# Two attention layers on one Trainium2 core: the first layer's projection steps as one stream, matrix work in program order, and edits to the order around them

## The chip, the cores and the metric

The kernel runs on one core of one Trainium2 chip. The metric is the device time of one execution in microseconds (us), lower is better. The engines of the core work beside each other, each on its own list of instructions in a fixed order: TensorE (PE in the rows, with its weight loads as PEld), VectorE (DVE), ScalarE (ACT), GpSimd (POOL) and SyncE (SP), which here does nothing but issue DMAs.

## What is computed

A decoder of two layers on 512 tokens of width 1024, in float32. The first layer ("fox") is causal attention with a learned decay, the second is latent attention (MLA) with rotary parts; each is followed by a gated feed-forward block.

```python
def fox_attention(xn, w_in, b_f, w_o):
    proj = xn @ w_in                      # q, k, v of 16 heads of 64, and a forget gate
    ...
    log_f = jax.nn.log_sigmoid(f_logit.astype(jnp.float32))
    cum = jnp.cumsum(log_f, axis=1)
    o = causal_block_attention(q, k, v, 1.0 / math.sqrt(FOX_HEAD_DIM), cum)
    return o.reshape(B, S, FOX_WIDTH) @ w_o
```

`causal_block_attention` is q·k times a scale, plus the difference of the two cumulated decays, masked, through a softmax over the keys, times v. The MLA layer does the same without the decay; its q and k have 96 columns a head, of which 32 are rotated.

## The kernel before

**Number format.** Each float32 matrix is held as a sum of two reduced-precision parts, hi and lo. A product is three matmuls (`mm3`, lines 375 to 378: hi·hi, hi·lo, lo·hi). The hi part of a weight is a cast on ACT (line 201), its lo part a subtraction (line 202) on DVE or, for the second half of a shared weight, on POOL. Weights come by one DMA of 512 KB each (line 238, SP's queue).

**A fox head.** Heads come in eight pairs (pair 0 to 7; heads 2p and 2p+1 are pair p). For the head *n*, `attention` (line 497) issues the scores of head *n*+1 first, then transposes of the softmax blocks of head *n* (`T_FIRST`, seven 128x128 blocks), then one dense step, then the last three blocks (`T_LAST`), the rest of the dense steps, and the products with V (`values`, eight matmuls into tile `o`). The softmax of a head is, for each of four blocks of rows, a maximum (DVE, line 439), an exponential (ACT, line 445), a reciprocal (DVE, line 452) and a multiplication (POOL line 454, DVE line 457 for the wider parts). A transposed block goes into its hi part (ACT, line 473) and its lo part (DVE, line 474). `o` is drained by ACT (line 486) and DVE (`oraw`, line 487). `T_LAST` and `o` share one PSUM buffer, so that `T_LAST` of a head can start only when `oraw` of the head before has been read out.

**The dense steps beside the heads ("fills").** While the heads run, PE also computes what later heads need. A pair's q and its k are a unit each, of four steps of six matmuls 512 wide (`qk_units`, line 714; tile `qkp`). Behind the fourth step of a unit `qk_parts` (line 694) makes its float32 form (DVE, `qf`, line 696), its hi part (ACT, line 698), its lo part (DVE, line 699) into a tile `hl` that has two buffers, and copies these by DMA from SP (lines 706 and 707 for q, 709 and 710 for k) into the operand tile `qk` of each of the two heads; two small rows of decay follow (lines 691 and 692). There are three `qk` tiles, used in turn. The scores of head 2p therefore need: the last matmul of pair p's k, then DVE, ACT, DVE, SP and the landing of the DMA. A V unit (eight steps of 12 matmuls 256 wide, from `v_unit`) serves four heads and is made in pairs 3 and 5. In the tail the output projection (`out_step`, line 548) fills the place of the q and k steps, as `wo` matmuls.

**What sets the order.** `distribute` (line 489) puts the steps of pair p into the heads 2p-3 and 2p-2, in equal shares. The order on each engine is then made by the scheduler of the framework: within PE, too, it can move an instruction ahead of one that stands earlier in the program. In before, this is what happens: the scores of the next pair, which the program writes right behind `values`, stand on PE some 6 us of work behind the last step of that pair's k. In the MLA layer a part of each head (lines 522 to 534) has a written order on ACT and DVE.

Of the kernel before, what the change touches and what calls it, by code (L numbers as in the profile page):

```python
# [9 lines left out]
F32 = mybir.dt.float32  # L10
F32R = mybir.dt.float32r
# [3 lines left out]
ALU = mybir.AluOpType  # L15
AX = mybir.AxisListType

P = 128
S = 512
# [143 lines left out]
def yoco_fox_mla_kernel(  # L163
# [325 lines left out]
    def distribute(fills, steps, at):  # L489

        share = sum(c for c, _ in steps) / len(at)
        done = 0.0
        for c, f in steps:
            fills.setdefault(at[min(int((done + 0.5 * c) / share), len(at) - 1)], []).append(f)
            done += c

    def attention(att, order, passes, v, oT, fills, split_softmax):

        n_heads = 2 * len(order)
        att.scores(passes(0))
        att.softmax((0, 1))
        att.softmax((3, 2))
        for f in fills.get(-1, []):
            f()
        for n in range(n_heads):
            p, hb = divmod(n, 2)
            more = n + 1 < n_heads
            if more:  # L510
                att.scores(passes(n + 1))
            att.transposes(T_FIRST)
            beside = fills.get(n, [])
            if more and split_softmax:
                att.softmax((0, 1))
            for f in beside[:1]:
                f()

            if split_softmax or not more:
                att.transposes(T_LAST)  # L520
                if more:
                    att.softmax((3, 2))
            else:
                att.softmax((0,))
                att.maximum(3)
                with tc.manual_schedule(engines={mybir.EngineType.Activation, mybir.EngineType.DVE}):
                    att.transposes(T_LAST)
                    att.maximum(1)
                    att.exponential(1)
                    att.exponential(3)  # L530
                    att.maximum(2)
                    att.exponential(2)
                for qb in (1, 3, 2):
                    att.normalise(qb)
            for f in beside[1:]:
                f()
            if hb == 0:
                oraw = tmp_tile("oraw")
            att.values(v(n), oraw, hb)
            if hb == 1:  # L540
                pp = order[p]
                ACT.copy(out=oT[:, 0, pp, :], in_=oraw)
                (POOL if more else DVE).tensor_tensor(
                    out=oT[:, 1, pp, :], in0=oraw, in1=oT.bitcast(F32)[:, 0, pp, :], op=ALU.subtract)
        for f in fills.get(n_heads, []):
            f()

# [126 lines left out]
    with ExitStack() as fx:  # L674
# [39 lines left out]
        def qk_units(pp, seq):  # L714
            steps = []
            for w, key in enumerate(("q", "k")):
                st = {}
                for c in range(4):
                    def go(c=c, w=w, key=key, st=st):
                        if c == 0:  # L720
                            st["w"] = getw((key, pp))
                            st["o"] = bank(ps_mm, "qkp")
                        dense(st["o"], st["w"], xs, [2 * c, 2 * c + 1], c == 0, c == 3)
                        if c == 3:
                            qk_parts(pp, seq, w, st["o"])
                    steps.append((6 * 0.216, go))
            return steps

        def run(steps):
            for _, f in steps:  # L730
                f()
# [65 lines left out]
            decay_rows(qk[hb].bitcast(F32), 2 * FOX_PAIRS[0] + hb)  # L797
        run(v1[7:])
        ahead = qk_units(FOX_PAIRS[1], 1)
        run(ahead[:2])  # L800

        oT = new_xs("oT_fox")
        wo_open = {}
        fills = {}
        for p in range(1, NPAIR):
            steps = ahead[2:] if p == 1 else qk_units(FOX_PAIRS[p], p)
            if p in (3, 5):
                qd = (p + 1) // 2
                steps += v_unit(lambda hf, q_=FOX_QUADS[qd]: ("v", q_, hf), xs, KT, 2, vts[qd], vtiles, norm)
            distribute(fills, steps, [-1, 0] if p == 1 else [2 * p - 3, 2 * p - 2])  # L810
        for at, m, c0, c1 in ((13, 0, 0, 6), (14, 1, 0, 6), (15, 0, 6, 7), (15, 1, 6, 7), (15, 2, 0, 2), (16, 2, 2, 5)):
            fills.setdefault(at, []).append(out_step("fwo", wo_open, oT, FOX_PAIRS, m, c0, c1))

        def fox_passes(n):
# [111 lines left out]
    with ExitStack() as fx:  # L926
# [54 lines left out]
        def rope_keys(krf):  # L981
            r = slice(0, ROPE)
            sw = tmp_tile("sw")
            DVE.stream_shuffle(sw[r], krf[r], SWAP)
            POOL.tensor_tensor(out=sw[r], in0=sw[r], in1=rope_s[r], op=ALU.mult)
            DVE.tensor_tensor(out=krf[r], in0=krf[r], in1=rope_c[r], op=ALU.mult)
            DVE.tensor_tensor(out=krf[r], in0=krf[r], in1=sw[r], op=ALU.add)
            krs = mp.tile([P, 2, S], F32R, name="krs", tag="rr", bufs=1)
            ACT.copy(out=krs[r, 0, :], in_=krf[r])
            DVE.tensor_tensor(out=krs[r, 1, :], in0=krf[r], in1=krs.bitcast(F32)[r, 0, :], op=ALU.subtract)  # L990
            for q in range(2):
                SP.dma_start(out=kr.bitcast(F32)[q * 64:(q + 1) * 64, :],
                             in_=krs.bitcast(F32)[r, q:q + 1, :].broadcast_to([ROPE, 2, S]))
# [87 lines left out]
        def rope_unit(qd):  # L1081
            def done(o):
                raw = tmp_tile("qr")
                if qd == 0:
                    DVE.tensor_tensor(out=raw, in0=o, in1=state["qrow"], op=ALU.mult)
                else:
                    ACT.copy(out=raw, in_=o)
                sw = tmp_tile("sw")
                DVE.stream_shuffle(sw, raw, SWAP)
                POOL.tensor_tensor(out=sw, in0=sw, in1=rope_s, op=ALU.mult)  # L1090
                DVE.tensor_tensor(out=raw, in0=raw, in1=rope_c, op=ALU.mult)
                DVE.tensor_tensor(out=raw, in0=raw, in1=sw, op=ALU.add)
                rr = mp.tile([P, 2, S], F32R, name="rr", tag="rr", bufs=1)
                ACT.copy(out=rr[:, 0, :], in_=raw)
                DVE.tensor_tensor(out=rr[:, 1, :], in0=raw, in1=rr.bitcast(F32)[:, 0, :], op=ALU.subtract)
                state["rr"] = rr
            return uq_unit(qd, 2, done)
# [22 lines left out]
        for p in range(1, NPAIR):  # L1120
# [17 lines left out]
                fills[11] = steps_f(uv[2:])  # L1138
                continue
            distribute(fills, steps, [-1, 0] if p == 1 else [2 * p - 3, 2 * p - 2])  # L1140
        for at, m, c0, c1 in ((12, 0, 0, 4), (13, 0, 4, 6), (13, 1, 0, 2), (14, 1, 2, 6), (15, 0, 6, 7), (15, 1, 6, 7),
                              (15, 2, 0, 2), (16, 2, 2, 5)):
            fills.setdefault(at, []).append(out_step("mwo", wo_open, oT, range(NPAIR), m, c0, c1))

# [130 lines left out]
```

## Time and profile before

| | |
|---|---|
| time, median of three runs | 1227.26 us (1226.89 to 1228.17) |
| the profiled execution | 1227.15 us |
| its span (first to last instruction in the profile) | 1225.4 us |
| PE busy in the span | 1211.3 us (99%) |
| DVE, ACT, POOL busy | 721.5 us (59%), 532.3 us (43%), 232.7 us (19%) |
| stretch of the fox heads | about 46 to 236 us |
| stretch of the MLA heads | about 670 to 824 us |

The profiled execution's time is 1.75 us longer than its span, and 0.11 us under the median of the runs. Busy times of PE are modelled a little long: a row can end after the next row of the same engine starts, so that distances between starts tell more than busy shares. In a timeline row the number in front is the start, then comes the length, the engine, the line and what is written and read; a bracket at the end is the engine's idle time before the row, and what released it.

### The profile page before, as it was taken

What the parts mean: (1) busy time and instruction counts of PE and PEld (TensorE: products, weight loads), DVE (VectorE), ACT (ScalarE), POOL (GpSimd) and SP (SyncE); (2) the same over time, 40 slices, a digit from 0 to 9 for tenths busy, and PEclk for the clock granted to TensorE, in tenths of its full rate; (3) what the DMA queues carried; (4) which work ended last, traced back from release to release, by engine and by line L of the source; (5) the groups of instructions that cost most, each with busy time, mean ns of one, the idle gap of its engine ahead of it and who ended that gap; (6) DMA issues with size and microseconds to landing.
All of it is one profiled execution on the core that took longest, in us unless ns stands there. A gap on an engine that the chain in (4) does not pass through costs nothing.

```text
span 1225.4 us, 16578 instructions
## 1 busy us (share of the span) xinstructions
PE 1211.3 (99%) x5959; PEld 1018.0 (83%) x5959; DVE 721.5 (59%) x1497; ACT 532.3 (43%) x1149; POOL 232.7 (19%) x268
## 2 busy tenths in 40 slices
PE   9999999999999999999999999999999999999997
PEld 7889888788888888888898888888888888888886
DVE  7776777645454554633467899967454545552323
ACT  6565556533233232322363577755333333332322
POOL 2333323211111111000012233322011111110100
PEclk9999999999999999999999999999999999999999
DMA  7554644223333323333324767714323232323322
GB/s 243 131 148 122 154 112 116 86 86 103 93 97 103 101 89 97 103 95 95 106 76 118 184 173 180 183 60 125 99 88 100 89 103 87 103 87 102 95 78 69
DMA packets 49890, 137.23 MB, mean 112 GB/s; under 512 B 5840, under 2 KB 10960, under 8 KB 49808
## 3 DMA queue, kind: packets, MB, share of 16 engines
q1 hardware_dynamic: 47264, 134.31, 38.1%
q10 hardware_dynamic: 2544, 1.87, 0.5%
q8 instruction: 47, 0.77, 0.3%
q14 instruction: 35, 0.29, 0.1%
HBM read 104.30 MB, written 2.10 MB: 87 GB/s over the span
## 4 chain that ended last, share of the span: by engine, by line
PE 93%; DVE 2%; DMA 2%; ACT 1%; issue 1%; POOL 1%; SPq 0%; ACTq 0%; POOLq 0%; DVEq 0%
PE dn L378 19%; PE dn L376 19%; PE dn L377 18%; PE s L427 4%; PE dn L1208 3%; PE dn L1207 3%; PE dn L1209 3%; PE o L483 3%; PE t L469 3%; PE qkp L376 2%; PE qkp L378 2%; PE qkp L377 2%; PE vv L586 1%; PE vv L585 1%; PE vv L584 1%
## 5 line engine op out<-in xcount | busy, mean ns | idle before, releaser
L201 ACT CAST whi<-wstage 128x512 fp32r<-128x512 f32 (+2 forms) x382 | 212.2, 601 | 450.5 <-issue 237.2
L202 DVE TENSOR_TENSOR wlo<-wstage,whi 128x512 fp32r<-128x512 f32 (+2 forms) x364 | 280.1, 805 | 111.4 <-ACT whi L201 111.2
L376 PE MATMUL dn<-xs,whi 128*128 128x512 f32 x704 | 275.1, 391 | 0.0
L378 PE MATMUL dn<-xs,wlo 128*128 128x512 f32 x704 | 274.0, 389 | 0.0
L377 PE MATMUL dn<-xs,whi 128*128 128x512 f32 x704 | 273.9, 389 | 0.0
L378 PEld LDWEIGHTS dn<-xs,wlo 128*128 128x128 f32 x704 | 132.1, 188 | 27.7
L376 PEld LDWEIGHTS dn<-xs,whi 128*128 128x128 f32 x704 | 132.2, 188 | 27.1
L377 PEld LDWEIGHTS dn<-xs,whi 128*128 128x128 f32 x704 | 132.2, 188 | 27.0
L857 POOL TENSOR_TENSOR u<-u,g 128x512 f32<-128x512 f32 x44 | 68.8, 1564 | 424.9 <-DVE u L856 379.6
L856 DVE TENSOR_TENSOR u<-dn,inv_row 128x512 f32<-128x512 f32 x44 | 30.4, 691 | 146.9 <-PE dn L378 146.9
L454 POOL TENSOR_SCALAR p<-p,rs 128x128 f32<-128x128 f32 (+1 forms) x128 | 63.6, 503 | 153.0 <-DVE rs L452 134.5
L445 ACT ACTIVATE p<-s,nm 128x512 f32<-128x512 f32 (+3 forms) x128 | 67.0, 529 | 38.5 <-DVE nm L439 31.3
L853 DVE TENSOR_TENSOR g<-dn,inv_row 128x512 f32<-128x512 f32 x44 | 30.4, 691 | 68.7 <-PE dn L378 68.7
L439 DVE CUSTOM_DVE_ANT_0 s<-s,mask 128x128 f32<-128x128 f32 (+3 forms) x128 | 61.0, 499 | 9.8 <-PE s L427 9.8
L340 POOL TENSOR_TENSOR acc<-acc,sq 128x512 f32<-128x512 f32 x22 | 33.2, 1507 | 161.4 <-ACT sq L339 161.2
L474 DVE TENSOR_TENSOR pt<-t,pt 128x384 fp32r<-128x384 f32 (+1 forms) x96 | 54.2, 593 | 7.4 <-ACT pt L473 6.8
L473 ACT CAST pt<-t 128x384 fp32r<-128x384 f32 (+1 forms) x96 | 46.6, 519 | 17.5 <-PE t L469 17.1
L376 PE MATMUL qkp<-xs_fox,whi 128*128 128x512 f32 x128 | 52.3, 409 | 0.0
L378 PE MATMUL qkp<-xs_fox,wlo 128*128 128x512 f32 x128 | 50.3, 393 | 0.0
L377 PE MATMUL qkp<-xs_fox,whi 128*128 128x512 f32 x128 | 49.8, 389 | 0.0
L469 PE MATMUL t<-ident,p 128*128 128x128 f32 x320 | 47.0, 274 | 2.4 <-POOL p L454 1.4
L469 PEld LDWEIGHTS t<-ident,p 128*128 128x128 f32 x320 | 38.2, 140 | 12.5 <-POOL p L454 3.7
(283 smaller groups left out, 2327.7 us busy)
## 6 DMA issues: line engine op xcount, KB each, us to landing
wstage<-in_weights SPq DMA_DIRECT2D x160, 512.0 KB
qk<-hl SPq DMA_DIRECT2D x32, 256.0 KB
mqk<-hl SPq DMA_DIRECT2D x16, 512.0 KB
wstage<-in_weights SPq DMA_DIRECT2D x16, 448.0 KB
wstage<-in_weights SPq DMA_DIRECT2D x10, 576.0 KB
qk<-hl SPq DMA_DIRECT2D x32, 128.0 KB
mqk<-rr SPq DMA_DIRECT2D x32, 128.0 KB
mqk<-hl SPq DMA_DIRECT2D x16, 256.0 KB
```

The source lines that it names most:

```text
L201: ACT.copy(out=hi[:, a:b], in_=stage[:, a:b])
L202: (POOL if shared and a else DVE).tensor_tensor(out=lo[:, a:b], in0=stage[:, a:b], in1=hi.bitcast(F32)[:, a:b], op=ALU.subtract)
L376: PE.matmul(o, lhsT=wh, rhs=xh, start=start, stop=False)
L377: PE.matmul(o, lhsT=wh, rhs=xl, start=False, stop=False)
L378: PE.matmul(o, lhsT=wl, rhs=xh, start=False, stop=stop)
L427: PE.matmul(t[:, off:off + n], lhsT=a[:, qb * P:(qb + 1) * P], rhs=b[:, 0:n], start=(i == 0), stop=(i == len(passes) - 1))
L439: DVE.tensor_tensor_reduce(out=sv, in0=sv, in1=mask[:, S - n:S], scale=1.0, scalar=BIG, op0=ALU.add, op1=ALU.min, accum_out=self.small[1][ ...
L445: ACT.activation(out=pv, in_=sv, func=AF.Exp, bias=nm[:, qb:qb + 1], scale=-1.0, accum_out=ssum[:, qb:qb + 1])
L454: POOL.tensor_scalar(out=pv[:, :cut], in0=pv[:, :cut], scalar1=r, scalar2=1.0, op0=ALU.mult, op1=ALU.mult)
L469: PE.transpose(t[:, i * P:(i + 1) * P], self.p[:, POFF[qb] + kb * P:POFF[qb] + (kb + 1) * P], ident)
L474: DVE.tensor_tensor(out=self.pt[1][:, sl], in0=t[:, :n], in1=self.pt[0].bitcast(F32)[:, sl], op=ALU.subtract)
L857: POOL.tensor_tensor(out=u, in0=u, in1=g, op=ALU.mult)
```

## The change

- The fox layer's steps of q, k and V are one list. Three steps (two before) of pair 1 run ahead of the heads; the others are dealt to the heads -1 to 12 by a fixed table of counts, 4 4 4 4 5 6 7 6 5 7 6 6 3 2, so that most pairs are made earlier than before.
- All of `attention` is under a manual schedule for PE: PE runs in the order in which the program is written. The other engines stay with the scheduler, but for two parts of the MLA heads.
- In the fox layer, where a head has four steps or more, two of them (one before) stand ahead of `T_LAST`.
- The output projection's steps are cut anew in both layers and begin in head 12 of fox.
- In the MLA layer, the split of a pair's output (`split_out`) comes a head later, and on POOL behind the first normalisation of the softmax; the head before the last takes the fox form of the softmax.
- Two rotary buffers become double, and a parameter for a scratch size goes from 1024 to 512.

```diff
+    def attention(*args):
+        with tc.manual_schedule(engines={mybir.EngineType.PE}):
+            attention_heads(*args)
...
+        def split_out(oraw, pp, eng):
+            ACT.copy(out=oT[:, 0, pp, :], in_=oraw)
+            eng.tensor_tensor(out=oT[:, 1, pp, :], in0=oraw, in1=oT.bitcast(F32)[:, 0, pp, :], op=ALU.subtract)
...
-            if more and split_softmax:
+            in_parts = split_softmax or n == n_heads - 2
+            if more and in_parts:
                 att.softmax((0, 1))
-            for f in beside[:1]:
+            ahead = 2 if split_softmax and len(beside) >= 4 else 1
+            for f in beside[:ahead]:
                 f()
...
-                att.softmax((0,))
+                att.maximum(0)
+                att.exponential(0)
+
+                with tc.manual_schedule(engines={mybir.EngineType.Pool}):
+                    att.normalise(0)
+                    if late is not None:
+                        split_out(*late)
+                        late = None
...
-            if hb == 1:
-                pp = order[p]
-                ACT.copy(out=oT[:, 0, pp, :], in_=oraw)
-                (POOL if more else DVE).tensor_tensor(
-                    out=oT[:, 1, pp, :], in0=oraw, in1=oT.bitcast(F32)[:, 0, pp, :], op=ALU.subtract)
+            if hb == 1 and more and not split_softmax:
+                late = oraw, order[p], POOL
+            elif hb == 1:
+                split_out(oraw, order[p], POOL if more else DVE)
...
-        run(ahead[:2])
+        run(ahead[:3])
...
-        for p in range(1, NPAIR):
-            steps = ahead[2:] if p == 1 else qk_units(FOX_PAIRS[p], p)
+
+        steps = ahead[3:]
+        for p in range(2, NPAIR):
+            steps += qk_units(FOX_PAIRS[p], p)
             if p in (3, 5):
...
-            distribute(fills, steps, [-1, 0] if p == 1 else [2 * p - 3, 2 * p - 2])
-        for at, m, c0, c1 in ((13, 0, 0, 6), (14, 1, 0, 6), (15, 0, 6, 7), (15, 1, 6, 7), (15, 2, 0, 2), (16, 2, 2, 5)):
+        for at, n in enumerate((4, 4, 4, 4, 5, 6, 7, 6, 5, 7, 6, 6, 3, 2)):
+            fills[at - 1] = [f for _, f in steps[:n]]
+            steps = steps[n:]
+        assert not steps
+        for at, m, c0, c1 in ((12, 0, 0, 3), (13, 0, 3, 6), (13, 1, 0, 3), (14, 1, 3, 5), (14, 1, 5, 6), (14, 0, 6, 7), (15, 1, 6, 7), (15, 2, 0, 2), (16, 2, 2, 5)):
...
-            krs = mp.tile([P, 2, S], F32R, name="krs", tag="rr", bufs=1)
+            krs = mp.tile([P, 2, S], F32R, name="krs", tag="rr", bufs=2)
...
-                rr = mp.tile([P, 2, S], F32R, name="rr", tag="rr", bufs=1)
+                rr = mp.tile([P, 2, S], F32R, name="rr", tag="rr", bufs=2)
```

In the rows of the instruction orders below, a name's number tells tiles of one name apart; numbers of before and of the change don't correspond. A row with x4 stands for four alike.

PE, where pair 7's k (`qkp`) ends and head 14's scores (`s` from `qk2`) come, before:

```order
L378 MATMUL qkp_2282<-xs_fox_130,wlo_2170 128x512
L483 MATMUL o_2337<-pt0_274,v_1771 128x512
...
L469 MATMUL t_2360<-ident_83,p_276 128x128 x4
L469 MATMUL t_2367<-ident_83,p_276 128x128 x3
L376 MATMUL wo_2392<-oT_fox_637,whi_2276 128x512
...
L469 MATMUL t_2411<-ident_83,p_276 128x128 x3
L427 MATMUL s_2349<-qk2_264 128x256 x4
```

PE at the same place in the change:

```order
L469 MATMUL t_2303<-ident_83,p_276 128x128 x3
L376 MATMUL qkp_2235<-xs_fox_130,whi_2123 128x512
...
L378 MATMUL qkp_2235<-xs_fox_130,wlo_2124 128x512
L376 MATMUL wo_2346<-oT_fox_643,whi_2229 128x512
...
L483 MATMUL o_2357<-pt0_274,v_1773 128x512
...
L427 MATMUL s_2369<-qk2_264 128x256 x4
```

Before, eight matmuls of `o`, seven transposes, 18 matmuls of `wo` and three more transposes stand between the two; in the change nine matmuls of `wo` and the eight of `o`.

PE, where pair 2's k ends and head 4's scores (`s` from `qk1`) come, before (`qkp_951` is k of pair 2, `qkp_1061` q of pair 3):

```order
L378 MATMUL qkp_951<-xs_fox_130,wlo_839 128x512
L483 MATMUL o_1006<-pt0_274,v_279 128x512
...
L469 MATMUL t_1036<-ident_83,p_276 128x128 x3
L376 MATMUL qkp_1061<-xs_fox_130,whi_945 128x512
...
L469 MATMUL t_1068<-ident_83,p_276 128x128 x3
L376 MATMUL qkp_1061<-xs_fox_130,whi_945 128x512
...
L427 MATMUL s_1018<-qk1_263 128x256 x4
```

PE at the same place in the change (`qkp_888` is k of pair 2, `qkp_999` q of pair 3):

```order
L469 MATMUL t_955<-ident_83,p_276 128x128 x3
L376 MATMUL qkp_888<-xs_fox_130,whi_776 128x512
...
L378 MATMUL qkp_888<-xs_fox_130,wlo_777 128x512
L376 MATMUL qkp_999<-xs_fox_130,whi_882 128x512
...
L469 MATMUL t_1006<-ident_83,p_276 128x128 x3
L376 MATMUL qkp_999<-xs_fox_130,whi_882 128x512
...
L483 MATMUL o_1035<-pt0_274,v_279 128x512
...
L427 MATMUL s_1047<-qk1_263 128x256 x4
```

`T_LAST` (three transposes) now stands behind twelve matmuls of steps where six stood, and `o` ahead of the scores comes behind it.

DVE, where pair 6's k is drained, before:

```order
L457 TENSOR_SCALAR p_276<-p_276,rs_2048 128x384
L452 RECIPROCAL rs_2048<-ssum_2046 128x1
L457 TENSOR_SCALAR p_276<-p_276,rs_2048 128x256
L696 TENSOR_TENSOR qf_2106<-qkp_2065,inv_row_397 128x512
L202 TENSOR_TENSOR wlo_2387<-wstage_2167,whi_2386 128x512 x2
L699 TENSOR_TENSOR hl_2108<-qf_2106,hl_2108 128x512
```

DVE at the same place in the change (line 717 is the former 696, line 720 the former 699):

```order
L474 TENSOR_TENSOR pt1_275<-t_2086,pt0_274 128x384
L717 TENSOR_TENSOR qf_2108<-qkp_2018,inv_row_397 128x512
L452 RECIPROCAL rs_2065<-ssum_2063 128x1
L202 TENSOR_TENSOR wlo_2341<-wstage_2121,whi_2340 128x512
L457 TENSOR_SCALAR p_276<-p_276,rs_2065 128x384
L202 TENSOR_TENSOR wlo_2341<-wstage_2121,whi_2340 128x512
L720 TENSOR_TENSOR hl_2110<-qf_2108,hl_2110 128x512
```

A reciprocal and a multiplication of the softmax now stand between `qf` and the lo part of `hl`; before, they stood ahead of `qf`.

## Rows read from the trace of the kernel before

**Rows 1.** The chain that ended last, share of the span by engine.

```profile
PE 93%; DVE 2%; DMA 2%; ACT 1%; issue 1%; POOL 1%; SPq 0%; ACTq 0%; POOLq 0%; DVEq 0%
```

**Rows 2.** Stretches: length, then busy PE, PEld, DVE, ACT, POOL, clock, DMA share, GB/s.

```profile
46.00:236.00 190.00, 187.76 (x1065) 161.47 (x1064) 140.36 (x365) 113.92 (x279) 64.90 (x89) 1.00 0.45 115
670.00:824.00 154.00, 151.91 (x878) 130.83 (x877) 136.14 (x385) 102.87 (x273) 46.12 (x75) 1.00 0.62 156
```

**Rows 3.** Waits of PE from 46 to 236 us: total us, times, longest.

```profile
PE t L469 <- DVE oraw L487: 0.8, 3, 0.3
PE t L469 <- POOL p L454: 0.6, 1, 0.6
PE s L427 <- issue: 0.5, 2, 0.2
```

**Rows 4.** Timeline, pair 2's last k matmul (80.16) to the scores of head 4.

```profile
80.16 0.39 PE L378 MATMUL qkp<-xs_fox,wlo 128*128 128x512 f32 x1
80.39 1.44 PE L483 MATMUL o<-pt,v 128*128 128x512 f32 x8
80.58 0.69 DVE L696 TENSOR_TENSOR qf<-qkp,inv_row 128x512 f32<-128x512 f32 x1 [1.08 <-PE qkp L378]
81.58 1.44 POOL L202 TENSOR_TENSOR wlo<-wstage,whi 128x512 fp32r<-128x512 f32 x1 [1.84 <-ACT whi L201]
81.66 0.93 PE L469 MATMUL t<-ident,p 128*128 128x128 f32 x7
82.05 1.51 DVE L699 TENSOR_TENSOR hl<-qf,hl 128x512 fp32r<-128x512 f32 x1 [0.18 <-ACT hl L698]
...
83.58 0.40 PE L378 MATMUL qkp<-xs_fox,wlo 128*128 128x512 f32 x1
83.59 1.32 SPq L709 DMA_DIRECT2D qk<-hl  x2
84.22 0.55 PE L469 MATMUL t<-ident,p 128*128 128x128 f32 x3 [0.24 <-DVE oraw L487]
...
85.74 1.13 SPq L238 DMA_DIRECT2D wstage<-in_weights  x1
...
86.44 0.39 PE L378 MATMUL qkp<-xs_fox,wlo 128*128 128x512 f32 x1
87.08 1.31 PE L427 MATMUL s<-qk 128*128 128x256 f32 x7 [0.24 <-issue]
```

**Rows 5.** Timeline, pair 6: its last k matmul drained, to the scores of head 12.

```profile
178.84 0.69 DVE L696 TENSOR_TENSOR qf<-qkp,inv_row 128x512 f32<-128x512 f32 x1 [1.10 <-PE qkp L378]
179.45 1.28 DVE L202 TENSOR_TENSOR wlo<-wstage,whi 128x512 fp32r<-128x512 f32 x2
...
180.66 0.68 DVE L699 TENSOR_TENSOR hl<-qf,hl 128x512 fp32r<-128x512 f32 x1
...
185.17 1.06 PE L427 MATMUL s<-qk 128*128 128x256 f32 x6
```

**Rows 6.** Timeline of an MLA head near the layer's end (POOL, DVE, PE).

```profile
798.62 1.28 POOL L543 TENSOR_TENSOR oT_mla<-oraw,oT_mla 128x512 fp32r<-128x512 f32 x1 [2.15 <-ACT oT_mla L542]
...
798.92 0.16 DVE L452 RECIPROCAL rs<-ssum 128x1 f32<-128x1 f32 x1
...
799.88 0.37 POOL L454 TENSOR_SCALAR p<-p,rs 128x128 f32<-128x128 f32 x1
...
800.30 0.33 PE L469 MATMUL t<-ident,p 128*128 128x128 f32 x1 [0.85 <-POOL p L454]
...
802.11 0.43 DVE L457 TENSOR_SCALAR p<-p,rs 128x384 f32<-128x384 f32 x1
```

**Rows 7.** A stretch after PE's last matmul (columns as in Rows 2).

```profile
1221.00:1222.00 1.00, 0.00 (x0) 0.00 (x0) 0.36 (x1) 0.39 (x1) 0.00 (x0) 0.62 0.00 0
```

**Rows 8.** Timeline of PE, the first matmuls of the program.

```profile
1.25 5.36 PE L298 MATMUL pg<-warm 128*128 128x512 bf16 x13 [1.25 <-DVE warm L285]
```

More of the change, by code (lines that the diff above doesn't have):

```diff
@@ L495, in distribute, with attention_heads @@
             done += c
-    def attention(att, order, passes, v, oT, fills, split_softmax):
+    def attention(*args):
+        with tc.manual_schedule(engines={mybir.EngineType.PE}):
+            attention_heads(*args)
+    def attention_heads(att, order, passes, v, oT, fills, split_softmax):
         n_heads = 2 * len(order)
+        late = None
+        def split_out(oraw, pp, eng):
+            ACT.copy(out=oT[:, 0, pp, :], in_=oraw)
+            eng.tensor_tensor(out=oT[:, 1, pp, :], in0=oraw, in1=oT.bitcast(F32)[:, 0, pp, :], op=ALU.subtract)
         att.scores(passes(0))
@@ L513, in attention @@
             beside = fills.get(n, [])
-            if more and split_softmax:
+            in_parts = split_softmax or n == n_heads - 2
+            if more and in_parts:
                 att.softmax((0, 1))
-            for f in beside[:1]:
+            ahead = 2 if split_softmax and len(beside) >= 4 else 1
+            for f in beside[:ahead]:
                 f()
-            if split_softmax or not more:
+            if in_parts or not more:
                 att.transposes(T_LAST)
@@ L522, in attention @@
                     att.softmax((3, 2))
-            else:
-                att.softmax((0,))
+                if late is not None:
+                    split_out(*late)
+                    late = None
+            else:
+                att.maximum(0)
+                att.exponential(0)
+                with tc.manual_schedule(engines={mybir.EngineType.Pool}):
+                    att.normalise(0)
+                    if late is not None:
+                        split_out(*late)
+                        late = None
                 att.maximum(3)
-                with tc.manual_schedule(engines={mybir.EngineType.Activation, mybir.EngineType.DVE}):
+                with tc.manual_schedule(engines={mybir.EngineType.Activation, mybir.EngineType.DVE, mybir.EngineType.PE}):
                     att.transposes(T_LAST)
@@ L534, in attention @@
                     att.normalise(qb)
-            for f in beside[1:]:
+            for f in beside[ahead:]:
                 f()
@@ L1140, in yoco_fox_mla_kernel @@
             distribute(fills, steps, [-1, 0] if p == 1 else [2 * p - 3, 2 * p - 2])
-        for at, m, c0, c1 in ((12, 0, 0, 4), (13, 0, 4, 6), (13, 1, 0, 2), (14, 1, 2, 6), (15, 0, 6, 7), (15, 1, 6, 7),
+        for at, m, c0, c1 in ((12, 0, 0, 2), (12, 0, 2, 4), (13, 0, 4, 6), (13, 1, 0, 2), (14, 1, 2, 4), (14, 1, 4, 6), (15, 0, 6, 7), (15, 1, 6, 7),
                               (15, 2, 0, 2), (16, 2, 2, 5)):
@@ L1257 @@
     from concourse.bass_utils import run_bass_kernel_spmd
-    nc = bacc.Bacc("TRN2", target_bir_lowering=False, num_devices=1, dynamic_dma_scratch_size=1024)
+    nc = bacc.Bacc("TRN2", target_bir_lowering=False, num_devices=1, dynamic_dma_scratch_size=512)
     arrays, args = {}, []
```

## The prediction

> **What bounds the kernel now.** I read first the chain that ended last: PE holds 93% of it [rows 1], so the time is the sum of PE's work plus the places where PE stands still. The change leaves every matmul in place (5935 before and after, the same shapes), so only the standing still can change. The windows say where it is: in the 190 us of the fox heads PE is not busy for 190 - 187.76 = 2.2 us, in the 154 us of the MLA heads for 154 - 151.91 = 2.1 us [rows 2]. That is a little too low, because busy rows overrun: the eight matmuls of `o` are 1.44 long but the transposes start 81.66 - 80.39 = 1.27 us after them [rows 4]. So each true wait costs its idle time and 0.17 more. All that the change could win in the two stretches is thus some 3 to 6 us. Next I read the waits by name: in fox PE waits for `oraw` ahead of `T_LAST` (three times, 0.8), for POOL's `p` (once, 0.6) and ahead of scores (twice, 0.5) [rows 3]. The last kind is the one that the change touches most, so I read the timeline of one instance.
>
> **The k chain.** Pair 2's last k matmul starts at 80.16, one matmul takes 80.39 - 80.16 = 0.23, so it is over at 80.39; the scores that need it start at 87.08 [rows 4]. On that path stand `qf` (80.58), a weight's lo part, `hl`'s lo part (82.05 to 83.56), the DMA (issued at 83.59) and 3.5 us to its landing. PE's last matmul ahead of the scores starts at 86.44 and should be followed after 0.23; the scores come after 0.64, so PE lost 0.41. The latency from the last k matmul to the scores is 87.08 - 80.39 = 6.7 us. Pair 6: `qf` at 178.84, as late after the matmul as above (80.58 - 80.39 = 0.19), so the matmul was over at 178.65 and the scores came at 185.17, 6.5 us later [rows 5]. I take **6.6 us** as the latency before.
>
> Against it stands what PE has to do between the two places. Before, for pair 7, that is eight `o`, ten transposes, 18 `wo` matmuls: 1.27 + 1.0 + 18 x 0.23 = 6.4 us, so nearly enough. In the program order of the change (the fences above, and likewise for the other pairs, taken from PE's order):
> - pair 1 and pair 2: 18 matmuls of steps, three transposes, `o`: 18 x 0.228 + 0.3 + 1.27 = 5.7 us;
> - pair 4 and pair 6: 18 matmuls and `o`: 4.1 + 1.27 = 5.4 us;
> - pair 7: nine `wo` matmuls and `o`: 2.05 + 1.27 = 3.3 us;
> - pair 3 and pair 5: over 13 us, since the V unit follows, so no wait.
>
> With 6.6 us as before, the waits are 0.9, 0.9, 1.2, 1.2 and 3.3, **7.5 us** in all.
>
> **What stands ahead in the queues.** The other engines' orders change too, and that moves the latency. At pair 6, a reciprocal and a 384 wide multiplication now stand between `qf` and the lo part: 0.16 + 0.43 [rows 6] = 0.6 more, so 7.2. Pair 7 has the same two rows, 7.1. At pair 2, ACT's hi part now comes behind an exponential that overwrites what `T_LAST` reads, and `T_LAST` now ends 6 matmuls plus itself after the last k matmul, 1.7 us; exponential 0.6, cast 0.6, the softmax multiplication and lo part behind: 7.5 by adding up. Pairs 1 and 4 gain little (6.7, 6.8). That adds 0.1 + 0.9 + 0.2 + 0.6 + 0.5 = **2.3 us**, so the waits are 9.8. The exponential and the cast are estimates, near the 0.69 of `qf`, which is of like width.
> Lower bound of the latency: with the lo part alone on DVE it takes 0.68 instead of 1.51 [rows 4, 5], so the 6.7 of pair 2 would be 5.9; waits of 0.2, 0.2, 0.5, 0.5, 2.6, 4.0 in all. Upper bound: at pair 2 a weight load now stands right ahead of the k copies on SP's queue; its issue takes 1.13 [rows 4], and I allow that once, 10.9 in all.
>
> The lo part at 82.05 is 1.51 long, ends 0.5 us after POOL's 1.44 that began at 81.58, and is 0.68 without POOL beside it [rows 4, 5]. The Trainium skill ("SBUF — State Buffer", section "Who interferes with whom") says that a DVE instruction with two inputs in SBUF contends with a GpSimd instruction that reads SBUF, and that the loser stands for the whole instruction. The trace agrees. By that rule pairs 6 and 7, whose weights are split on DVE alone, keep the short form, and pairs 1 and 4 the long one; the sum above would be the same with it, and 1.7 us lower if the rule failed at both.
>
> **What is removed.** The wait of `T_LAST` for `oraw`: two steps (12 matmuls, 2.7 us) ahead of it instead of one, together with scores and seven transposes more than the longest row needs; three waits of 0.8 + 3 x 0.17 = 1.3 us go [rows 3]. The two old waits of scores, 0.5 + 2 x 0.17 = 0.85, are replaced by the new ones and must be taken off. POOL's `p` in the tail, 0.6 + 0.17 = 0.77 [rows 3], goes, since the tail's `wo` steps are cut finer and spread. Together **-2.9**. In the tail's last head, `T` now follows shorter cover; I add 0.5 for it (bounds 0 and 0.77, the wait that stood there).
>
> **MLA.** PE's, ACT's and DVE's orders stay the same up to the last five heads, so the 2.1 us mostly stay. POOL's order changes: a pair's `oT` comes behind the first normalisation. Near the end `p` could have begun when its reciprocal was done, 798.92 + 0.16 = 799.08, but POOL was on `oT` (798.62 to 799.90) and began at 799.88; the transposes waited 0.85 [rows 6]. So 0.8 comes back: **-0.8** (bounds: -2.1, all of the stretch's idle time, and +1.0, if `oT` now comes late for what reads it). Double rotary buffers, scratch size, third step ahead of the heads: no row shows a wait on them, so 0; the third step needs its weight earlier, but the view of rows 3 names no wait for weights inside the heads.
>
> **Sum.** 9.8 - 2.9 + 0.5 - 0.8 = +6.6 us. The profiled execution's time is 1227.15 (span 1225.4 and 1.75 outside it), 0.11 under the median; 1227.15 + 6.6 = **1233.8 us**. A measurement of this kernel can tell about 0.2%, 2.45 us: faster is below 1224.8, slower above 1229.7.
>
> **Rivals.**
> 1. **Slower, as forecast**: the k chain is the new wait, 1229.7 to 1238. For it: the latency of 6.5 to 6.7 is alike at both pairs shown, and cover of 3.3 can't hide it. Against: the latency is itself a product of the queues, and these are less pressed when PE waits.
> 2. **Cancelled**: the latency falls to its lower bound 5.9, waits 4.0, and 4.0 - 2.9 + 0.5 - 0.8 = +0.8, so 1228. For it: DVE and ACT are busy 74% and 60% of the stretch [rows 2], so there is slack.
> 3. **Faster**: k's chain also jumps the queue (no weight's lo part ahead of it, 0.65 less [rows 5], 5.2): waits 1.9 at pair 7 and 0.0 elsewhere, and MLA gives back all its 2.1: 1.9 - 2.9 - 2.1 = -3.1, so 1224. It decides for faster from a latency of about 5.5 downwards. Against: the orders of DVE keep the weight's lo part in front.
> 4. **Slower still, by the clock**: the wait of pair 7, near 4 us, may cost PE its clock. At the end of the run the granted clock, 1.00 (2.4 GHz) in both stretches [rows 2], is 0.62 as the mean of a stretch in which PE had already stood still, on its way to the lower level of 1.2 GHz [rows 7]. Coming up again has its price: the first 13 matmuls take 5.36, where 13 x 0.23 = 3.0 would do [rows 8]; so +2.4, and 1236 (up to 1240 with the upper bounds).
> The Trainium skill ("TensorE: Matmul & The Clock Gate", section "HAM oscillation — how this bites in real kernels") says that a TensorE left idle goes to half its clock. The trace agrees at the end of the run only; inside the heads no wait of rows 3 to 6 is longer than 0.85 us, so no run of before shows it there.
> 5. **Not what it says**: if the other engines' queues already hid every step, the time would stay at 1227. The fences show that the order of PE does change, so this is part of rival 2.
>
> **Chances.** Forecast 0.55, clock 0.10, cancelled 0.18, faster 0.17. So faster 0.17, same 0.18, slower 0.65. The range leaves out most of the faster case and the far end of the clock's: 1224.5 to 1240.
>
> **What would show it.** Right: in the waits of PE from 46 to 240 us, "`s` behind a DMA or issue" becomes the first row, with about 10 us in five waits, the longest some 4 us ahead of head 14's scores; `T_LAST` behind `oraw` is gone. Rival 2: the same row with 4 us. Rival 3: no wait of scores but one, under 2 us. Clock: a stretch near 200 us with a granted clock under 1.00. MLA: the wait of 0.85 for POOL's `p` is gone. What would make me wrong first is the latency: if the DMA lands sooner, or `qf` no longer waits behind the softmax, each 0.5 us takes 2.5 off the sum.

## The result and the profile after

The changed kernel takes **1242.32 us** (median of four runs, 1241.92 to 1242.81) against 1227.32 us before: 1.0121 of the time before, with a 95% interval of 1.0109 to 1.0133. It is slower by 15.0 us. The prediction was slower by 6.6 us, 1233.8, with a range up to 1240: the sign is right, the size and the range are not. The profiled execution took 1242.81 us, its span is 1241.0, 15.6 more than before.

I read the same views again. First the chain that ended last (it answers to [rows 1]): PE has lost two points, DVE has gained two.

```profile
PE 91%; DVE 4%; DMA 2%; issue 1%; ACT 1%; POOL 0%; SPq 0%; DVEq 0%; POOLq 0%; ACTq 0%
```

Then the windows (they answer to [rows 2]; length, busy PE, PEld, DVE, ACT, POOL, clock, DMA share, GB/s):

```profile
46.00:236.00 190.00, 178.80 (x1006) 155.75 (x1005) 128.38 (x350) 103.67 (x264) 64.06 (x86) 0.96 0.44 112
...
670.00:824.00 154.00, 150.32 (x863) 130.55 (x861) 137.13 (x384) 100.38 (x264) 43.69 (x70) 1.00 0.67 168
```

In the fox heads PE now stands still for 190 - 178.8 = 11.2 us, where it was 2.2, and the granted clock of that stretch is 0.96 and no longer 1.00. So two things cost there, standing still and slow running; the busy column counts slow matmuls as busy and hides the second. The starts of two landmarks, the first scores of the MLA layer and the last matmul, share out the whole loss. Before:

```profile
682.94 0.36 PE L427 MATMUL s<-mqk 128*128 128x256 f32 x1 [0.69 <-DMA mqk<-hl]
...
1218.26 0.28 PE L1209 MATMUL dt<-whi,actB 128*128 128x256 f32 x1
```

In the change:

```profile
696.27 0.36 PE L427 MATMUL s<-mqk 128*128 128x256 f32 x1 [0.50 <-DMA mqk<-hl]
...
1233.84 0.28 PE L1235 MATMUL dt<-whi,actB 128*128 128x256 f32 x1
```

Up to the first scores of the MLA layer 13.3 us are lost, and behind them 2.2 us more.

The waits of PE by name (answering to [rows 3]; total us, times, longest; from 46 to 236 us):

```profile
PE s L427 <- DMA qk<-hl: 9.6, 4, 3.7
PE s L427 <- issue: 0.9, 1, 0.9
PE o L483 <- DVE pt L474: 0.7, 1, 0.7
```

Five waits of scores, 10.5 us idle, and nothing left of `oraw` or `p`: this is the picture that the prediction described. The five in order are the scores of the heads 2, 4, 8, 12 and 14, the first heads of the pairs 1, 2, 4, 6 and 7 (timelines of PE):

```profile
67.80 0.62 PE L427 MATMUL s<-qk 128*128 128x256 f32 x3 [0.77 <-DMA qk<-hl]
...
90.28 0.55 PE L427 MATMUL s<-qk 128*128 128x256 f32 x1 [3.51 <-DMA qk<-hl]
...
141.82 0.35 PE L427 MATMUL s<-qk 128*128 128x256 f32 x1 [0.85 <-issue]
...
191.77 0.48 PE L427 MATMUL s<-qk 128*128 128x256 f32 x2 [1.56 <-DMA qk<-hl]
...
212.06 0.55 PE L427 MATMUL s<-qk 128*128 128x256 f32 x1 [3.72 <-DMA qk<-hl]
```

With 0.17 for each, as in the prediction, they are 0.9, 3.7, 1.0, 1.7 and 3.9 us, 11.2 in all; forecast were 1.0, 1.8, 1.4, 1.8 and 3.8, together 9.8. Four of the five are right within 0.4 us; pair 2 is off by 1.9.

**Pair 2**, from the last k matmul to the scores of head 4 (it answers to [rows 4]):

```profile
80.29 0.39 PE L378 MATMUL qkp<-xs_fox,wlo 128*128 128x512 f32 x1
81.52 0.67 DVE L717 TENSOR_TENSOR qf<-qkp,inv_row 128x512 f32<-128x512 f32 x1
...
82.35 0.58 ACT L445 ACTIVATE p<-s,nm 128x384 f32<-128x384 f32 x1 [0.33 <-POOL p L454]
82.92 0.61 ACT L719 CAST hl<-qf 128x512 fp32r<-128x512 f32 x1
83.33 0.76 DVE L457 TENSOR_SCALAR p<-p,rs 128x256 f32<-128x256 f32 x1
83.96 0.34 SPq L238 DMA_DIRECT2D wstage<-in_weights  x1
84.01 0.68 DVE L720 TENSOR_TENSOR hl<-qf,hl 128x512 fp32r<-128x512 f32 x1
84.71 0.66 SPq L730 DMA_DIRECT2D qk<-hl  x1
```

The matmul is over at 80.29 + 0.23 = 80.52. The lo part of `hl` ends at 84.69, 4.2 us later: the queue of exponential, cast and softmax multiplication is much as it was added up (7.5 less 3.5 of DMA leaves 4.0). The lo part itself is short here (0.68, where [rows 4] has 1.51), and the queue ahead of it is what makes the time. But from the issue at 84.71 to the scores at 90.28 pass **5.6 us**, where it was 87.08 - 83.59 = 3.5 in [rows 4]. In front of the copy stands the 512 KB weight load, issued at 83.96.

**The clock.** Windows of 2 us behind the waits of head 4 and of head 14 (columns as above):

```profile
88.00:90.00 2.00, 0.00 (x0) 0.00 (x0) 0.10 (x1) 0.00 (x0) 0.00 (x0) 0.61 1.07 230
90.00:92.00 2.00, 1.72 (x7) 1.75 (x8) 0.36 (x2) 0.00 (x0) 0.00 (x0) 0.50 0.19 41
92.00:94.00 2.00, 2.00 (x9) 1.70 (x8) 1.62 (x6) 0.55 (x3) 0.03 (x1) 0.50 0.00 0
94.00:96.00 2.00, 2.00 (x9) 1.67 (x8) 1.49 (x5) 1.44 (x4) 0.42 (x2) 0.68 0.02 4
96.00:98.00 2.00, 2.00 (x12) 1.65 (x11) 1.50 (x3) 1.67 (x4) 1.09 (x2) 1.00 0.00 0
...
210.00:212.00 2.00, 0.00 (x0) 0.00 (x0) 0.00 (x0) 0.00 (x0) 0.00 (x0) 0.83 0.96 228
212.00:214.00 2.00, 1.95 (x7) 1.98 (x8) 0.43 (x3) 0.00 (x0) 0.00 (x0) 0.50 0.72 251
214.00:216.00 2.00, 2.00 (x10) 1.70 (x9) 1.77 (x7) 0.78 (x3) 0.26 (x1) 0.50 0.02 6
216.00:218.00 2.00, 2.00 (x7) 1.61 (x6) 1.26 (x4) 1.22 (x4) 0.42 (x2) 0.50 0.00 0
218.00:220.00 2.00, 2.00 (x11) 1.60 (x11) 0.00 (x0) 0.43 (x1) 0.18 (x1) 0.96 0.00 0
```

While PE stands still the clock goes to 0.50, the lower level of 1.2 GHz, and it stays there for some 5 to 6 us after PE has work again. So the clock fell twice, during the two waits of 3.5 and 3.7 us, and not at the 1.56 of head 12.

**MLA.** The waits of the MLA layer have another name than before (660 to 850 us):

```profile
PE o L483 <- DVE pt L474: 4.0, 4, 1.4
PE s L427 <- DMA mqk<-hl: 0.5, 1, 0.5
```

The wait for POOL's `p` [rows 6] is gone, as forecast. In its place the products with V wait, four times, for the lo part of the last transposed blocks. One of the four (POOL, DVE, DVE, PE):

```profile
812.47 1.28 POOL L510 TENSOR_TENSOR oT_mla<-oraw,oT_mla 128x512 fp32r<-128x512 f32 x1
...
812.48 1.82 DVE L202 TENSOR_TENSOR wlo<-wstage,whi 128x512 fp32r<-128x512 f32 x1
814.23 0.54 DVE L474 TENSOR_TENSOR pt<-t,pt 128x384 fp32r<-128x384 f32 x1
...
814.83 1.44 PE L483 MATMUL o<-pt,mv 128*128 128x512 f32 x7 [1.37 <-DVE pt L474]
```

DVE's lo part of a weight takes 1.82 here and not the 0.64 that each of two takes in [rows 5] (1.28 for both); the late `oT` on POOL began 0.01 us ahead of it. This is the contention that the prediction cited from the Trainium skill ("SBUF — State Buffer", section "Who interferes with whom"), at a place where it was not looked for. What this one is worth, and whether it is the cause of the four waits, the experiments below tell.

### The profile page after: what moved, and what is told of

It reads as the page before. It is cut to its first block, busy times and chain, and to the rows that moved or that the text cites. A ratio compares the mean times of both kernels' runs of the same rounds, so it can differ in the third digit from the quotient of the medians.

```text
span 1241.0 us, 16547 instructions
## 1 busy us (share of the span) xinstructions
PE 1215.6 (98%) x5959; PEld 1024.2 (83%) x5959; DVE 722.2 (58%) x1497; ACT 530.6 (43%) x1149; POOL 235.3 (19%) x268
## 4 chain that ended last, share of the span: by engine, by line
PE 91%; DVE 4%; DMA 2%; issue 1%; ACT 1%; POOL 0%; SPq 0%; DVEq 0%; POOLq 0%; ACTq 0%
PE dn L376 18%; PE dn L378 18%; PE dn L377 18%; PE s L427 4%; PE dn L1235 3%; PE dn L1234 3%; PE dn L1233 3%; PE o L483 3%; PE t L469 2%; PE qkp L376 2%; PE qkp L377 2%; PE qkp L378 2%; DMA qk<-hl 1%; PE uq L376 1%; PE uq L378 1%
## 5 line engine op out<-in xcount | busy, mean ns | idle before, releaser
L445 ACT ACTIVATE p<-s,nm 128x128 f32<-128x128 f32 (+3 forms) x128 | 67.5, 531 | 58.2 <-PE t L469 32.3
L439 DVE CUSTOM_DVE_ANT_0 s<-s,mask 128x512 f32<-128x512 f32 (+3 forms) x128 | 61.1, 499 | 18.0 <-PE s L427 17.8
```

What stands on the lines that cost most here:

```text
L439: DVE.tensor_tensor_reduce(out=sv, in0=sv, in1=mask[:, S - n:S], scale=1.0, scalar=BIG, op0=ALU.add, op1=ALU.min, accum_out=self.small[1][ ...
L445: ACT.activation(out=pv, in_=sv, func=AF.Exp, bias=nm[:, qb:qb + 1], scale=-1.0, accum_out=ssum[:, qb:qb + 1])
```

## Experiments

My theory after the result: fox loses 11.2 us because the k chain has too little PE work in front of its scores, and about 5 us more to the clock that falls behind the two longest of these waits; MLA loses its 2.2 us either to the late split or to PE's program order. Rivals: the clock's fall costs nothing on the path; the stream, or program order as such, is the cause in fox, so that other late inputs would take the place of k.

### Keeping PE busy through the two long waits

```diff
             if more:
+                if split_softmax and n in (3, 13):
+                    busy = bank(ps_t, "t")
+                    ka, kb_ = passes(n)[0]
+                    for _ in range(12):
+                        PE.matmul(busy, lhsT=ka[:, 0:P], rhs=kb_, start=True, stop=True)
                 att.scores(passes(n + 1))
```

> The change, with twelve more matmuls 512 wide (result read by nobody) put on PE ahead of the scores of head 4 and of head 14, where PE stood 3.5 and 3.7 us without work. They take 12 x 0.23 = 2.7 us of each wait, and the scores still come when their copies land. Theory (the two long waits cost their length and, on top, the granted clock that falls behind them, 2.7 and 3.1 us): the granted clock stays at 1.00 through both places, the scores start at the same time after their wait, and the time is 5.8 us lower, about 1236.5. Rival (the waits alone cost; the clock's fall is no loss on the path): the time stays at 1242 within 1 us.

Measured: 1237.90 us (1.0084 of before, 1.0069 to 1.0099), so 4.4 us less than the change, where 5.8 were expected. The windows at the same two places:

```profile
88.00:90.00 2.00, 1.93 (x9) 1.27 (x7) 0.54 (x1) 0.00 (x0) 0.00 (x0) 1.00 1.03 221
90.00:92.00 2.00, 1.38 (x9) 1.28 (x10) 0.63 (x3) 0.00 (x0) 0.00 (x0) 1.00 0.39 83
...
210.00:212.00 2.00, 1.88 (x13) 1.78 (x14) 1.13 (x5) 0.21 (x1) 0.00 (x0) 1.00 0.89 253
212.00:214.00 2.00, 2.00 (x12) 1.70 (x11) 2.00 (x8) 1.61 (x6) 0.37 (x1) 1.00 0.02 8
```

The clock stays at 1.00. The scores of head 4 are as late as before:

```profile
90.62 0.35 PE L427 MATMUL s<-qk 128*128 128x256 f32 x1 [0.69 <-DMA qk<-hl]
```

Of their wait 0.69 of idle time is left behind 12 x 0.23 = 2.7 of added matmuls, together 3.4, where it was 3.5. From the first scores to the end of the last `wo` matmul of fox the stretch is 184.4 us, with the change 189.6. So the clock's fall costs **about 5 us** (4.4 by the medians, 5.2 by this stretch), and the rival falls. Here useless work is faster than standing still.

### The copies of k ahead of the weight load

```diff
-        with tc.manual_schedule(engines={mybir.EngineType.PE}):
+        engines = {mybir.EngineType.PE}
+        if args[-1]:
+            engines.add(mybir.EngineType.SP)
+        with tc.manual_schedule(engines=engines):
             attention_heads(*args)
```

> The change with SP's DMAs, too, in the program's order in the fox heads, so that the copies of pair 2's k stand ahead of the weight load that the change has in front of them; the decay rows now stand with them. Theory (the copy, 5.6 us from issue to scores there instead of 3.5 elsewhere, is late because of the 512 KB in front of it): the wait of head 4's scores goes from 3.5 to about 1.5 us, the clock does not fall there, together 4.5 us less, about 1237.8. Rival (the landing is late whatever stands in front): 1242 within 1 us.

Measured: 1243.18 us (1.0125, 1.0110 to 1.0140): the time does not fall, and 1237.8 was expected. But the local step goes the way that the theory says. SP's queue and the scores of head 4:

```profile
85.32 0.61 SPq L733 DMA_DIRECT2D qk<-hl  x1
85.99 0.59 SPq L734 DMA_DIRECT2D qk<-hl  x1
...
87.37 0.68 SPq L716 DMA_DIRECT2D qk<-frows  x1
...
89.29 2.28 PE L427 MATMUL s<-qk 128*128 128x256 f32 x7 [1.92 <-DMA qk<-hl]
...
90.98 0.33 SPq L238 DMA_DIRECT2D wstage<-in_weights  x1
```

From the issue of the copy to the scores it is now 89.29 - 85.32 = 4.0 us and not 5.6, and the wait is 1.92 and not 3.51. The order of SP's queue is thus shown as the cause of most of pair 2's miss (1.6 of 2.1 us). The rest may be the decay rows: at each of the five heads the scores now come 1.9 to 2.0 us behind the issue of the second decay row (here 87.37 and 89.29), so they, and not the copies, seem to land last. What ate the gain are other waits (0.5 ahead of `o` shortly before, 1.2 for head 8 where it was 0.9, 4.0 for head 14 where it was 3.7), which leave 10.3 us of waits from 46 to 236 us where the change has 11.2, and the clock, which fell three times instead of twice: its mean over this stretch is 0.96, as in the change.

```profile
90.00:92.00 2.00, 2.00 (x8) 1.70 (x7) 0.98 (x4) 0.00 (x0) 0.00 (x0) 0.50 0.66 141
190.00:192.00 2.00, 1.38 (x6) 1.23 (x7) 0.40 (x2) 0.00 (x0) 0.00 (x0) 0.79 0.62 130
192.00:194.00 2.00, 2.00 (x9) 1.70 (x8) 1.49 (x6) 0.46 (x2) 0.00 (x0) 0.50 0.73 153
212.00:214.00 2.00, 0.98 (x4) 1.01 (x5) 0.00 (x0) 0.00 (x0) 0.00 (x0) 0.50 0.61 129
```

The clock fell at a wait of 1.9 us ahead of head 4 (with 0.5 more ahead of `o` shortly before) and right behind one of 1.7 us ahead of head 12. The expectation, a wait of about 1.5 us ahead of head 4 and no fall there, was wrong in both.

### Another table of counts

The first table that I tried was 5 4 4 4 4 8 8 4 4 8 8 5 3 0 in place of 4 4 4 4 5 6 7 6 5 7 6 6 3 2.

> The change with another table of counts, 5 4 4 4 4 8 8 4 4 8 8 5 3 0, so that the last step of each pair's k stands a head earlier: PE work between it and the scores 9.1, 10.4, 10.4, 11.8 and 7.0 us for the pairs 1, 2, 4, 6 and 7 instead of 5.7, 5.7, 5.4, 5.4 and 3.3. Theory (the time is lost because the k chain, 6.7 to 7.5 us long, has too little PE work in front of its scores): the five waits, 11.2 us, go but for some 0.3 at pair 7, the clock does not fall, another 5.8; the time is about 1225.5 (1224 to 1228). Rival (the stream as such is the cause, since a fixed PE order meets other late inputs: weights, transposed blocks, V): other waits take the place, and the time stays over 1233.

Measured: 1260.08 us (1.0265, 1.0250 to 1.0281). This kernel computes something else: the table moves the q of the pairs 2, 3, 5 and 7 ahead of the last scores that use the tile which it overwrites, so these scores take the new q, and must wait for its copy. It can't decide the question. All the same it agrees with the mechanism at a larger dose, since q's copies now have only the products with V (at pair 7 six matmuls besides) in front of the scores that take them: the waits of scores are 23.6 us, the longest 6.3, and the mean clock from 46 to 236 us is 0.94. The expectation's covers are those of the k copies alone.

The second table is 5 3 5 3 5 8 8 3 5 8 8 3 5 0, which keeps every q behind those scores.

```diff
-        for at, n in enumerate((4, 4, 4, 4, 5, 6, 7, 6, 5, 7, 6, 6, 3, 2)):
+        for at, n in enumerate((5, 3, 5, 3, 5, 8, 8, 3, 5, 8, 8, 3, 5, 0)):
```

> The change with the table of counts 5 3 5 3 5 8 8 3 5 8 8 3 5 0 and nothing else: each pair's k ends a head earlier, each q not before the last scores of the tile that it overwrites. PE work between k and scores: 7.7, 9.0, 9.0, 9.0 and 7.0 us for the pairs 1, 2, 4, 6 and 7. PE stays in program order. Theory (the latency of 6.5 to 9 us has to be covered): waits of under 1 us in all, no fall of the clock, about 1226.5. Rival (program order as such loses, other waits take the place): over 1233.

Measured: 1227.81 us (1.0004, 0.9994 to 1.0013), **14.5 us less** than the change, by nothing but the table. The waits of PE from 46 to 236 us:

```profile
PE o L483 <- DVE pt L474: 1.9, 2, 1.2
```

Not one wait of scores is left, and the clock doesn't fall. The waits are 1.9 us and not under 1, and the time is 1.3 over what was expected. PE in program order is not by itself the trouble in fox; the place of k in that order is. The waits of `o` that are left stand in the heads 12 and 14, which now have few steps of their own.

### The scheduler's order on PE in the fox heads

```diff
     def attention(*args):
+        if args[-1]:
+            return attention_heads(*args)
         with tc.manual_schedule(engines={mybir.EngineType.PE}):
```

> The change with PE's order in the fox heads left to the scheduler again (the MLA layer keeps the program's order); the stream of steps is that of the change. The scheduler puts 6.4, 8.1, 6.0, 6.8 and 6.9 us of PE work between the last k step and the scores of the pairs 1, 2, 4, 6 and 7, where the change has 5.7, 5.7, 5.4, 5.4 and 3.3. Theory (the wait is latency minus work in front): waits of some 2 us in all instead of 11.2, no fall of the clock (5 us), about 1228.5. Rival (the stream's early steps themselves load DVE, ACT and SP so that copies come later and later): waits over 6 us stay, and the time is over 1234.

Measured: 1228.50 us (1.0008, 0.9999 to 1.0017), as the theory said. Waits from 46 to 236 us:

```profile
PE s L427 <- DMA qk<-hl: 1.2, 2, 1.0
PE s L427 <- issue: 0.2, 1, 0.2
```

So the same stream, dealt with the same counts, costs next to nothing where the scores may move back by 1 to 4 us of work. The three kernels agree with one sum, wait = latency less work in front (pair 7, work and then wait with its 0.17: 3.3 and 3.9 in the change, 6.9 and 0.35 here, 7.0 and none with the second table).

### The late split of the MLA layer

```diff
-                with tc.manual_schedule(engines={mybir.EngineType.Pool}):
-                    att.normalise(0)
-                    if late is not None:
-                        split_out(*late)
-                        late = None
+                att.normalise(0)
...
-            if hb == 1 and more and not split_softmax:
-                late = oraw, order[p], POOL
-            elif hb == 1:
+            if hb == 1:
                 split_out(oraw, order[p], POOL if more else DVE)
```

> The change with the MLA layer's split of a pair's output where it was before (right behind the products with V, POOL's place left to the scheduler). Theory (the late split on POOL starts with, and lengthens, the weight's lo part that DVE has ahead of the transposed block's lo part, and so makes the products with V late): the waits of V products in the last MLA heads (1.3, 0.5, 1.4, 0.8) go and the older waits for POOL's p (0.8) come back; the time is 2 us lower, about 1240.3. Rival (PE's program order in the MLA layer costs that time): no change, 1242.3 within 0.7.

Measured: 1241.25 us (1.0110, 1.0093 to 1.0127), 1.1 less than the change; the intervals overlap. It is less than it seems: from the first MLA scores to the last matmul it takes 537.5 us, with the change 537.6, so nothing came from the MLA layer. The 1.1 us stand in the fox heads, which this edit doesn't touch: their wait for head 4 is 3.04 in place of 3.51, and behind the wait of head 14 (3.74, in the change 3.72) the granted clock is back at 1.00 in the window from 216 to 218 us, where the change has 0.50. So kernels with the same fox heads differ by a microsecond or two there, and only the stretch behind them tells of MLA. The waits of `o` fall from 4.0 to 3.2, yet the stretch is no shorter; what takes their place is not in the view of waits. My theory of the late split falls: DVE's long subtraction beside POOL is there at one place, but it isn't what the MLA layer lost.

### PE's order in the MLA layer left to the scheduler

```diff
     def attention(*args):
+        if not args[-1]:
+            return attention_heads(*args)
         with tc.manual_schedule(engines={mybir.EngineType.PE}):
```

> The change with PE's order in the MLA layer left to the scheduler again (but for the part written out at T_LAST); the fox heads keep the program's order. Theory (without the late split, waits of V products of 1.3, 0.5, 0.6 and 0.7 were left in the last MLA heads: in program order nothing else can run there, while before the scheduler put other matmuls in front): these shrink and the time is 1 to 2 us lower, about 1240.8. Rival (the MLA layer's loss is the late split alone, which was worth 1.1): no change, 1242.3 within 0.7.

Measured: 1238.09 us (1.0084, 1.0070 to 1.0097), 4.2 less than the change. From the first MLA scores to the last matmul it takes 534.2 us, **3.4 less** than with the change and 1.1 less than before (535.3); the rest stands, again, in the fox heads (the wait of head 4 is 2.82, and the clock is at 1.00 from 216 to 218 us). The waits from 660 to 850 us:

```profile
PE s L427 <- DMA mqk<-hl: 0.5, 1, 0.5
PE wo L377 <- POOL oT_mla L512: 0.5, 1, 0.5
PE t L469 <- POOL p L454: 0.2, 1, 0.2
```

No `o` waits for DVE any more. At the head of the `o` that was shown above (814.83 in the change), program order has six matmuls of `wo` between the last three transposes and `o`; here ten and one more transpose stand there. So program order is what the MLA layer lost.

### A version better than both, and one more

The fox layer of the change in program order with the second table, two more steps of the output projection in head 12, and the MLA layer as before the change (but for the two rotary buffers and the scratch size, which stay as in the change). Of its edit only the list of output steps is shown, and only its start.

```diff
-        ... ((12, 0, 0, 3), (13, 0, 3, 6), (13, 1, 0, 3), (14, 1, 3, 5), ...
+        ... ((12, 0, 0, 3), (12, 0, 3, 5), (13, 0, 5, 6), (13, 1, 0, 4), (14, 1, 4, 5), ...
```

> A version meant to be better than both: the fox layer of the change in PE's program order with the counts 5 3 5 3 5 8 8 3 5 8 8 3 5 0, two more steps of the output projection in head 12 (8.4 us of PE work ahead of head 14's scores), and the MLA layer as before the change. Theory: the fox heads lose 2 to 3 us less than before the change (no waits for oraw, none for scores), the MLA layer loses what it lost before: about 1224.5 (1223 to 1226), against 1227.3 before. Rival (fox in program order can't beat the scheduler): 1227.3 or more.

Measured: **1222.85 us** (0.9962 of before, 0.9950 to 0.9974), 4.5 us under before, 19.5 under the change, and a little below the expected range. The window of the fox heads has 0.15 us without work, and no wait of the view is left there:

```profile
46.00:236.00 190.00, 189.85 (x1079) 164.65 (x1079) 143.25 (x369) 115.23 (x284) 64.35 (x89) 1.00 0.47 121
```

The last kernel takes this version, with the MLA edits of the change instead, but not PE's program order there.

> The fox layer of the version that beat both (counts 5 3 5 3 5 8 8 3 5 8 8 3 5 0, five pairs' output steps in head 12), and the MLA layer of the change with PE's order left to the scheduler: the late split, POOL's written order and the recut output steps stay. It tells what the MLA edits are worth without PE's program order. Theory (the late split gives back POOL's wait of 0.8, as forecast; what the MLA layer of the change lost was PE's program order): 0.6 to 1.1 us under that version's 1222.85, about 1222.0. Rival (the MLA edits are worth nothing or cost, whatever orders PE): 1222.85 or more.

Measured: 1222.45 us (0.9959, 0.9946 to 0.9973). The two intervals overlap almost wholly, so 0.4 us in the time are not settled. From the first MLA scores to the last matmul it is 534.1 against 534.9: by the profile the MLA edits give 0.7 us if the scheduler orders PE, near the 0.8 that was forecast for them. The third step ahead of the heads, the double rotary buffers and the scratch size are in this kernel too, so they are not what the change lost.

## Why the prediction was wrong

Its steps in turn:

- **The bound.** Right in the main: PE decides the time, and its standing still moved most, as the chain, the windows and the waits by name told. But "only the standing still can change" is the step that failed: the same matmuls (5959 PE rows in both traces, not 5935) also ran slower, which was 5.2 of the 15.6 us.
- **Latency against work in front.** Right, and it carried the sign: 9.8 us of waits forecast, 11.2 measured, and the second table and the scheduler's order both take them away. The failed part is pair 2 (1.8 forecast, 3.7 measured); at pair 4 the lo part was counted at its long form and took 0.77, and the wait is 1.0 and not 1.4. The prediction saw that a weight load stands in front of its copies and left it out of the sum; as a bound it allowed the 1.13 us of that load's *issue*. What counts is the load's transfer: 5.6 us from the copy's issue to the scores in place of 3.5, and 4.0 with the load behind.
- **The clock.** This is the largest term that the sum left out. The forecast had a wait of 3.8 us ahead of head 14 and the row that shows the clock falling behind a standing PE [rows 7], and yet gave the fall a chance of 0.10, once, at 2.4 us. It fell twice and cost about 5: once at the wait that the forecast contained, and once at pair 2's, which it had at half its length. The price of a single fall was about right (2.2 to 2.6 measured); what failed is that the fall was weighed as an accident apart from the sum. With the one fall in it the sum would have been 9.8 + 2.4 - 2.9 + 0.5 - 0.8 = 9.0, so 1236.2, still inside the range and 6 us short. Whether pair 2's wait would have kept its clock at the forecast 1.8 us is not told by the change; with the copies in front the clock fell there at 1.92.
- **The rule on the clock.** The Trainium skill ("TensorE: Matmul & The Clock Gate", section "HAM oscillation — how this bites in real kernels") says that a TensorE left idle goes to half its clock, and the prediction found the trace of before to agree at the end of the run only. This trace agrees inside the heads too (0.50 behind waits of 3.5 and 3.7 us).
- **What is removed in fox.** Right in kind: the waits for `oraw` and `p` are gone [rows 3]. The better version shows their worth with nothing new in their place: its heads have 0.15 us without work in the window that had 2.2.
- **MLA.** Wrong sign: -0.8 forecast, +2.2 measured. The -0.8 holds by itself (0.7 by the profile of the last kernel). What failed is "PE's, ACT's and DVE's orders stay the same up to the last five heads, so the 2.1 us mostly stay": in those last heads the scheduler had reordered PE, and program order cost 3.4 us there.

Added up by the profiles: +11.2 (scores) + 5.2 (clock) - 3.1 (old waits, less what stands in the fox tail now, as the difference that is left to 13.3) + 3.4 (MLA in program order) - 1.1 (MLA edits: 534.2 with the scheduler's order against 535.3 before) = 15.6. Of the 9.0 us that this is over the forecast's 6.6, the clock is 5.2, MLA 3.0, the scores 1.4, and the rest -0.7. Without the clock's term, or without the miss in MLA, the time would have come out inside the range.

**What stays open.** How short a wait may be before the clock falls: 1.7 us was enough in one kernel, 1.56 was not in another. How long it then stays low: behind head 14's wait (3.72, 3.74 and 3.67 us in three kernels with the same fox heads) PE had some 6 us of work at the lower level in the change and some 3 in the others. Why pair 2's wait differs between these kernels (3.5, 3.0, 2.8): the copy took 5.6, 5.1 and 4.9 us from issue to scores, so the difference is in the transfer, but its cause wasn't tried. Whether the scheduler would do as well as program order with the second table wasn't tried either.

## What to carry to other kernels

When a hand-written order replaces a scheduler's, take each producer's latency from the trace and compare it with the work that the new order puts between its last instruction and the consumer (3.3 us of work against a latency of 7.1 was on the sheet here); one table of counts decided 14.5 us. Where the sum contains a wait of several microseconds of TensorE, put the clock's fall into the same sum, and where a DMA is in the chain, look at what stands in front of it on its queue and count that transfer, not its issue. A program order can be switched on for one stretch alone: here it went with the best time in fox and cost 3.4 us in MLA.

## What the runs showed of the hardware that I had not expected

- Behind a wait of 3.5 us the granted clock was 0.50 for 5 us of work after PE had started again. Two waits of 3.5 and 3.7 us cost about 5 us more by the clock. Twelve useless matmuls in each of the two brought 4.4 us back.
- In one kernel the clock fell at waits of 1.9 and 1.7 us, in another it did not at 1.56.
- A copy issued 0.75 us behind a 512 KB load on the same queue took 5.6 us to the scores that need it, at most 4.0 without it in front, and 3.5 in the kernel before.
- A DVE subtraction that takes 0.64 took 1.82 when a POOL subtraction of 1.28 had begun 0.01 us earlier. It took 1.05 where POOL's had begun 0.8 us earlier, in the kernel without the late split, and the MLA layer gained nothing by it.
